# Hybrid Hyena, mLSTM and S5 block on one core: S5 tables at two places, modulation on ScalarE, and the output order

## The chip, the cores and the metric

The kernel runs on one core of one Trainium2 chip, as one launch. The core has TensorE (matmuls and transposes), VectorE, ScalarE, GpSimd and SyncE, each with its own instruction queue that is worked off in order, and DMA queues that SyncE, ScalarE and GpSimd issue transfers on. The metric is the device time of one launch in microseconds (us); smaller is better. In the rows of the profile PE is TensorE's matmuls, PEld its weight loads, DVE VectorE, ACT ScalarE, POOL GpSimd and SP SyncE.

## The reference

One layer of a hybrid backbone, for 256 latent tokens `x` and 256 context tokens `ctx`, width D = 2048, all in fp32. Cut to what the change touches:

```
mod_l = split(silu(c) @ w_mod + b_mod, 6);  mod_c = split(silu(c_ctx) @ w_mod + b_mod, 6)
h_ctx = ctx * (1 + mod_c[1]) + mod_c[0];    h_lat = x * (1 + mod_l[1]) + mod_l[0]
hy, qk, v, o, gates, u, mg = split(h @ w_in)          # widths 2304, 1536, 768, 768, 16, 768, 6144
y_hy = hyena(hy)          # short convolution, then two long convolutions
y_ml = mlstm(qk, v, gates, o)
# S5: 48 groups of 16 channels, 64 complex states each, both directions, context first, then latents
s[t] = A_bar * s[t-1] + B_bar @ u[t];   y[t] = Re(C @ s[t])
y_s5 = z * sigmoid(z @ glu_w + glu_b),  z = gelu(y + d * u)
merged = sigmoid(mg[0]) * (y_hy @ w_hy_out) + sigmoid(mg[1]) * (y_ml @ w_ml_out) + sigmoid(mg[2]) * (y_s5 @ w_s5_out)
x = layer_norm(alpha * x + mod_l[2] * (merged @ w_out))
out = layer_norm(alpha * x + mod_l[5] * mlp(x * (1 + mod_l[4]) + mod_l[3]))
```

S5 is computed by chunks of 8 tokens, 64 chunks in all. `WA` holds the powers of A_bar times B_bar, which take the inputs of a chunk to its end state (the inject); the scan runs over the 64 chunks; `QD` holds the powers times C, which take a chunk's start state to its outputs; `KD` holds the lag kernels (C, powers, B), which take the inputs of a chunk to its own outputs.

## The kernel before

Each large matmul is fp32 made of three products of a rounded format: the weight chunk `wr` (128 x 1024, loaded on SyncE's queue, four buffers) is split by ScalarE into `wh` (a copy, L190) and by VectorE into `wl` (a subtraction, L194), three buffers each; `mm` (L211) then issues 24 matmuls of 256 columns for a chunk, 48 where it serves latents and context. A tile scheduler, which has a cost model of its own, sets the order in which each engine's instructions stand; the code gives it priorities by its own order. Side work is written as generators: `with_side` starts one, `chunk_done` advances each by its rate at every chunk, `drain` runs one out.

The stages, by the times of the profiled execution:

- First stage (`phase0`, scope `p0a`, to about 235 us): eight `mod_block`s multiply `w_mod` by `silu(c)` (matmuls `px`, L406) into `modc`. `h_group` (L435) modulates x and ctx in place, 32 pieces of 128 x 256 on VectorE, and splits them into the operands `t`. K steps of `w_in` run between. On the side: `s5_params` (L443) computes A_bar's powers `s5pq` and B_bar, and `s5_tables` the tables. `powers` makes them with broadcast products (L536, L537) and one sum (L538), direction 0 on VectorE and direction 1 on GpSimd; `s5Q` is C's table, `s5w` B's. L564 multiplies `s5Q` by B (`s5bb`) for the lag kernels. QD, KK and WA go to memory.
- pA, to about 582 us: at its start a copy `gate` on GpSimd and `s5_spread`, which writes KK into the 8 block-diagonal places of KD; then V, Q, mLSTM, U, O columns, with the Hyena filters and the later modulation (`mod_late`: `mac`, L1181) beside them. `u_consume` puts U into UD (memory) and `uT`.
- pB, to about 980 us: 6 steps of the Hyena columns `hy`, `s5_inject` (WA and UD loaded on ScalarE's queue, L634 matmuls, results to `S`), then `s5_scan` as a side: 63 steps of four GpSimd operations (L652 to L655) on 128 x 96, each needing the one before. Beside it stand 36 `hy` steps with their short convolutions (L741, L743) and 32 steps of the gate columns `mg`. `s5_output` (L687 on) needs the scan's end; 48 gate-column steps, and the gated unit `s5_glu`.
- pC: `hyena` with the last 16 gate-column steps, and the merges; then `w_out`, norms, and the MLP to 2044 us.

## Time and profile before

| | |
|---|---|
| median of 3 runs | 2034.3 us (2031.83 to 2036.18) |
| the profiled execution | 2046.25 us, its span 2044.3 us |
| granted TensorE clock, mean over the span | 0.964 |
| busy in the span: TensorE, VectorE, ScalarE, GpSimd | 1885.0, 1342.6, 797.7, 473.4 us |
| DMA | 455.92 MB, 223 GB/s |

TensorE is busy 92% of the span, so most stages are bound by its matmuls. A stage with another limit shows where TensorE's share falls; so the profile is read by stretches below. A wait is put down to the engine and line that released it last. Where transfers are the subject, the DMA share and GB/s of a stretch count, and what SyncE's queue waited for.

### The profile page before, as it was taken

What the parts mean: (1) busy time and instruction counts of PE and PEld (TensorE: products, weight loads), DVE (VectorE), ACT (ScalarE), POOL (GpSimd) and SP (SyncE); (2) the same over time, 40 slices, a digit from 0 to 9 for tenths busy, and PEclk for the clock granted to TensorE, in tenths of its full rate; (3) what the DMA queues carried; (4) which work ended last, traced back from release to release, by engine and by line L of the source; (5) the groups of instructions that cost most, each with busy time, mean ns of one, the idle gap of its engine ahead of it and who ended that gap; (6) DMA issues with size and microseconds to landing.
All of it is one profiled execution on the core that took longest, in us unless ns stands there. A gap on an engine that the chain in (4) does not pass through costs nothing.

```text
span 2044.3 us, 34693 instructions
## 1 busy us (share of the span) xinstructions
PE 1885.0 (92%) x13945; PEld 1716.5 (84%) x13945; DVE 1342.6 (66%) x1842; ACT 797.7 (39%) x1079; POOL 473.4 (23%) x654
## 2 busy tenths in 40 slices
PE   4787899999999896999889998899999999999996
PEld 1555888898998896999769977899989899998986
DVE  8789876655876564455777767866655555555556
ACT  1233333324544332534333443544343334444332
POOL 4777311000015997000343400500000000000001
PEclk8898899999999898999999999999999999999998
DMA  8798667766698675777756876577765566666653
GB/s 311 262 299 285 195 203 221 228 199 184 206 318 272 211 242 172 262 251 243 270 183 217 278 249 218 174 248 229 244 208 190 189 185 181 184 185 230 190 187 115
DMA packets 255200, 455.92 MB, mean 223 GB/s; under 512 B 28789, under 2 KB 75541, under 8 KB 253504
## 3 DMA queue, kind: packets, MB, share of 16 engines
q1 hardware_dynamic: 221824, 382.43, 59.0%
q0 software_dynamic: 12384, 44.54, 6.2%
q10 hardware_dynamic: 20832, 26.75, 3.9%
q8 instruction: 109, 1.79, 0.4%
q14 instruction: 51, 0.42, 0.1%
HBM read 424.75 MB, written 32.05 MB: 223 GB/s over the span
## 4 chain that ended last, share of the span: by engine, by line
PE 64%; DVE 14%; DMA 8%; POOL 8%; issue 4%; ACT 1%; ACTq 0%; POOLq 0%; DVEq 0%; SPq 0%
PE mm L211 57%; DMA wr<-in_w_mod_dram 4%; PE aux L211 4%; DVE wl L194 4%; POOL sc L654 2%; POOL sc L653 2%; POOL t L655 2%; POOL sc L652 2%; DVE t L194 1%; DMA wr<-in_w_in_dram 1%; DVE ty L435 1%; ACT wh L190 1%; DVE mac L1181 1%; DVE s5t L537 1%; DMA s5wq<-WA 1%
## 5 line engine op out<-in xcount | busy, mean ns | idle before, releaser
L211 PE MATMUL mm<-t,wh 128*128 128x256 f32 x5888 | 1102.7, 288 | 24.8 <-ACT wh L190 12.6
L211 PEld LDWEIGHTS mm<-t,wh 128*128 128x128 f32 x5888 | 933.7, 194 | 46.6 <-ACT wh L190 13.9
L194 DVE TENSOR_TENSOR wl<-wr,wh 128x1024 fp32r<-128x1024 f32 (+1 forms) x517 | 657.0, 1277 | 381.6 <-ACT wh L190 380.7
L211 PE MATMUL mm<-t,wl 128*128 128x256 f32 x2944 | 850.1, 289 | 23.3 <-DVE wl L194 23.0
L190 ACT ACTIVATE wh<-wr 128x1024 fp32r<-128x1024 f32 (+1 forms) x517 | 546.4, 1058 | 807.9 <-PE mm L211 577.6
L211 PEld LDWEIGHTS mm<-t,wl 128*128 128x128 f32 x2944 | 571.4, 194 | 37.4 <-DVE wl L194 29.4
L1181 DVE SCALAR_TENSOR_TENSOR mac<-wr,vecs,mac 128x512 f32<-128x512 f32 x240 | 186.8, 778 | 152.7 <-DMA wr<-in_w_mod_dram 150.0
L211 PE MATMUL mm<-wh,t 128*128 128x512 f32 (+1 forms) x960 | 249.3, 349 | 1.7 <-ACT wh L190 1.7
L211 PEld LDWEIGHTS mm<-wh,t 128*128 128x128 f32 x960 | 169.7, 191 | 25.6 <-ACT wh L190 2.7
L211 PE MATMUL mm<-wl,t 128*128 128x512 f32 (+1 forms) x480 | 169.2, 352 | 5.2 <-DVE wl L194 5.2
L211 PE MATMUL mm<-wh,ff 128*128 128x512 f32 (+1 forms) x576 | 155.3, 358 | 0.0
L211 PEld LDWEIGHTS mm<-wh,ff 128*128 128x128 f32 x576 | 101.8, 188 | 17.6
L211 PEld LDWEIGHTS mm<-wl,t 128*128 128x128 f32 x480 | 91.6, 191 | 21.7 <-DVE wl L194 10.5
L211 PE MATMUL mm<-wl,ff 128*128 128x512 f32 (+1 forms) x288 | 103.0, 357 | 0.0
L1403 POOL DMA_DIRECT2D t<-in_ln_g_dram x1 | 0.5, 535 | 358.8 <-PE mm L211 358.8
L211 PE MATMUL mm<-ty,wh 128*128 128x256 f32 x384 | 74.1, 291 | 0.0
L211 PE MATMUL mm<-ty,wl 128*128 128x256 f32 x192 | 57.0, 297 | 6.7 <-DVE wl L194 6.7
L211 PEld LDWEIGHTS mm<-ty,wh 128*128 128x128 f32 x384 | 61.6, 195 | 0.9
L211 PEld LDWEIGHTS mm<-wl,ff 128*128 128x128 f32 x288 | 54.2, 188 | 8.8
L1192 POOL DMA_DIRECT2D mrow<-b x8 | 4.0, 502 | 227.8 <-DVE b L1190 227.8
L211 PE MATMUL aux<-t,t 128*128 128x384 f32 (+3 forms) x160 | 48.8, 422 | 8.0 <-DVE t L1147 3.5
L406 PE MATMUL px<-wr,b 128*32 128x512 f32 x128 | 40.3, 714 | 12.9 <-DVE s5t L335 10.7
(389 smaller groups left out, 1813.6 us busy)
## 6 DMA issues: line engine op xcount, KB each, us to landing
wr<-in_w_ff_dram SPq DMA_DIRECT2D x256, 512.0 KB, 3.9
wr<-in_w_in_dram SPq DMA_DIRECT2D x192, 512.0 KB, 4.7
wr<-in_w_mod_dram SPq DMA_DIRECT2D x160, 512.0 KB, 4.8
wr<-in_w_out_dram SPq DMA_DIRECT2D x32, 512.0 KB, 4.9
wh<-in_w_mod_dram SPq DMA_DIRECT2D x16, 512.0 KB, 6.2
wl<-in_w_mod_dram SPq DMA_DIRECT2D x16, 512.0 KB, 7.8
QD<-s5Q POOLq DMA_DIRECT2D x24, 256.0 KB, 4.9
WA<-s5wa ACTq DMA_DIRECT2D x24, 256.0 KB, 5.2
```

The lines of the kernel that those rows point to most:

```text
L190: return self.nc.scalar.activation(out, in_, f, bias=bias, scale=scale)
L194: self.nc.vector.tensor_sub(lo, x, hi.bitcast(F32))
L211: self.nc.tensor.matmul(out, lhsT, rhs, start=start, stop=stop, skip_group_check=True)
L406: nc.tensor.matmul(ps[o:o + 32], self.st[:, k, :], raw[:, kk, :], start=k < 4, stop=k >= KT - 4, skip_group_check=True, tile_position=(0, o))
L435: self.nc.vector.tensor_scalar(h[:, j], h[:, j], self.modc[:, 16 + k, m:m + 1], self.modc[:, k, m:m + 1], op0=ALU.mult, op1=ALU.add)
L537: e.tensor_mul(t[:, :, s], bcp(s), bcm(1))
L652: v.tensor_mul(t1, self.a8[:, 0], S[:, :, :, :, n - 1])
L653: v.tensor_mul(t2, self.a8[:, 1], S[:, :, ::-1, :, n - 1])
L654: v.tensor_add(t1, t1, S[:, :, :, :, n])
L655: v.tensor_add(S[:, :, :, :, n], t1, t2)
L1181: v.scalar_tensor_tensor(acc, x, c, acc, op0=ALU.mult, op1=ALU.add)
L1192: nc.gpsimd.dma_start(self.mrow[which // 3:which // 3 + 1, o:o + 512], brow)
```

## The change

`h_group` modulates on ScalarE (an Identity activation with a per-partition scale and bias). `s5_tables` is split in two. `s5_into` stays in the first stage: the powers of B, their transposes and WA. The new `s5_tables` makes Q, the lag kernels and KK in a new scope `pT`, beside the Hyena and gate columns, at the rate 0.6, and at its end calls `s5_spread`, which no longer stands in pA. All powers are on VectorE, four state pairs at a time: products of 512 (B) or 576 (C), and one sum of twice that. B and the powers `s5pq` are written to memory (SB, PQ) and loaded again. QD and KK are written on ScalarE's queue.

`s5_inject` takes one pair at a time: 24 loads of WA of 256 KB on GpSimd's queue, four buffers. UD, KD, QD and the new UL, which keeps U in memory in place of `uT`, are loaded on GpSimd's queue too. mLSTM's `st_all` becomes four smaller tiles, so that it no longer waits for the tile that the modulated inputs hold.

The order changes too: 4 `hy` steps before the inject rather than 6; then the scan and the tables beside 36 `hy` and 24 gate-column steps, the tables run out, 8 more gate-column steps, `s5_output` at the rate 0.4 with 24 steps beside it, and 40 steps left for the Hyena stage.

```diff
@@ h_group
-                    self.nc.vector.tensor_scalar(h[:, j], h[:, j], self.modc[:, 16 + k, m:m + 1],
-                                                 self.modc[:, k, m:m + 1], op0=ALU.mult, op1=ALU.add)
+                    self.act(h[:, j], h[:, j], AF.Identity, bias=self.modc[:, k, m:m + 1],
+                             scale=self.modc[:, 16 + k, m:m + 1])
@@ s5_params, its end
+        nc.gpsimd.dma_start(self.SB, B.rearrange("p a b c -> p (a b c)"))
+        nc.gpsimd.dma_start(self.PQ, pq.rearrange("p a b c -> p (a b c)"))
@@ powers
-        e = self.nc.vector if d == 0 else self.nc.gpsimd
...
+        v = self.nc.vector
+        q = slice(24 * d + 4 * ct, 24 * d + 4 * ct + 4)
...
         for s in range(2):
-            e.tensor_mul(out[:, :, s], bcp(1 + s), bcm(0))
-            e.tensor_mul(t[:, :, s], bcp(s), bcm(1))
-        e.tensor_add(out, out, t)
+            v.tensor_mul(out[:, s], bcp(1 + s), bcm(0))
+            v.tensor_mul(t[:, s], bcp(s), bcm(1))
+        v.tensor_add(out, out, t)
+    def s5_into(self):
+        for ct in range(CT):
+            wt = []
+            for d in range(2):
+                w = self.t(self.br, [P, 2, 4, P], "s5w", 4)
+                self.powers(w.rearrange("p s q (l c) -> p s q l c", c=16), self.s5B, d, ct, d, LC)
+                wt.append(w)
+            yield
+            for i in range(4):
+                wa = self.t(self.br, [P, 4, P], "s5wa", 2)
+                pt = self.aux([P, 4, P])
+                for d in range(2):
+                    for s in range(2):
+                        self.tr(pt[:, 2 * d + s, :], wt[d][:, s, i])
+                self.act(wa, pt)
+                nc.scalar.dma_start(self.WA[ct, :, i], wa)
+                if i % 2:
+                    yield
     def s5_tables(self):
+        nc.gpsimd.dma_start(B.rearrange("p a b c -> p (a b c)"), self.SB)
+        nc.gpsimd.dma_start(self.pq.rearrange("p a b c -> p (a b c)"), self.PQ)
+        nc.gpsimd.dma_start(C, self.I["s5c"])
         for ct in range(CT):
...
+            for d in range(2):
+                Q = self.t(self.br, [P, 2, 4, 144], "s5Q", 2)
+                self.powers(Q.rearrange("p s q (l c) -> p s q l c", c=16), C, d, ct, 0, 9)
+                bb = self.t(self.br, [P, 2, 4, 32], "s5bb", 2)
+                nc.gpsimd.memset(bb, 0.0)
...
-                    nc.gpsimd.dma_start(self.QD[ct, d, :, 2 * half:2 * half + 2], Q[:, :, :, o:o + P])
+                nc.scalar.dma_start(self.QD[ct, d], Q[:, :, :, o:o + P])
...
-            nc.gpsimd.dma_start(self.KK[ct], kk.rearrange("p l c -> p (l c)"))
+            nc.scalar.dma_start(self.KK[ct], kk.rearrange("p l c -> p (l c)"))
+        self.s5_spread()
@@ s5_inject
-            wa = self.t(self.br, [P, 4, 4, P], "s5wq", 2)
-            nc.scalar.dma_start(wa, self.WA[ct])
...
+            for i in range(4):
+                wa = self.t(self.br, [P, 4, P], "s5wa", 4)
+                nc.gpsimd.dma_start(wa, self.WA[ct, :, i])
@@ mlstm
-        st_all = self.t32(F32, (P, 4, HEADS, T))
-            s_sb = st_all[:, sb]
+            s_sb = self.ty()[:, :HEADS, :]
@@ run
-                    yield from self.s5_tables()
+                    yield from self.s5_into()
...
-                gate = self.t(self.sm, [P, LC], "gate", 1)
-                nc.gpsimd.tensor_copy(gate[:LC], self.kT[:LC, 2, :LC])
-                nc.gpsimd.dma_start(self.KD[:, 0, 0, 0, 0].unsqueeze(1), gate[:LC, 0:1])
-                self.s5_spread()
...
-                self.run_steps(hy, 6)
-                self.s5_inject()
+                self.run_steps(hy, 4)
+                for _ in self.s5_inject():
+                    pass
                 self.sides[1][1] = 0.3
                 self.with_side(self.s5_scan(), 2)
+                self.with_side(self.s5_tables(), 0.6, 2)
                 self.run_steps(hy, 36)
-                self.run_steps(steps, 32)
-                self.with_side(self.s5_output(), 0.6)
-                self.run_steps(steps, 48)
+                self.run_steps(steps, 24)
+                self.drain(2)
+            with self.scope("pB") as self.br:
+                self.run_steps(steps, 8)
+                self.with_side(self.s5_output(), 0.4)
+                self.run_steps(steps, 24)
```

On VectorE in the first stage, around a modulated group, the order before is this (`s5Q`, `s5w` and `s5t` are the tables and their products, `ty` the inputs, `t_19` and `t_20` the split operands):

```order
L537 TENSOR_TENSOR s5t_31_129<-s5pq_189,s5B_121 128x2x128 x2
L415 TENSOR_TENSOR modc_101<-px_457,vecs_93 128x8
L538 TENSOR_TENSOR s5w_418<-s5w_418,s5t_31_129 128x512
L435 TENSOR_SCALAR ty_107<-ty_107,modc_101 128x256 x2
L435 TENSOR_SCALAR ty_109<-ty_109,modc_101 128x256 x2
L435 TENSOR_SCALAR ty_108<-ty_108,modc_101 128x256 x2
L435 TENSOR_SCALAR ty_110<-ty_110,modc_101 128x256 x2
L537 TENSOR_TENSOR s5t_31_129<-s5pq_189,s5C_122 128x2x144 x2
L194 TENSOR_TENSOR t_19_102<-ty_107,t_19_102 128x512
L194 TENSOR_TENSOR wl_559<-wr_556,wh_558 128x1024
```

And after it:

```order
L539 TENSOR_TENSOR s5w_360<-s5w_360,s5t_130 128x1024
L538 TENSOR_TENSOR s5t_130<-s5pq_190,s5B_124 128x512 x2
L539 TENSOR_TENSOR s5w_366<-s5w_366,s5t_130 128x1024
L194 TENSOR_TENSOR t_22_105<-ty_110,t_22_105 128x512
L194 TENSOR_TENSOR t_23_106<-ty_112,t_23_106 128x512
L538 TENSOR_TENSOR s5t_130<-s5pq_190,s5B_124 128x512 x2
L194 TENSOR_TENSOR wl_513<-wr_510,wh_512 128x1024
L194 TENSOR_TENSOR t_22_105<-ty_111,t_22_105 128x512
L194 TENSOR_TENSOR t_23_106<-ty_113,t_23_106 128x512
L537 TENSOR_TENSOR s5w_416<-s5pq_190,s5B_124 128x512 x2
L537 TENSOR_TENSOR s5w_422<-s5pq_190,s5B_124 128x512 x2
```

The modulations and `s5Q` are gone from there, and a `powers` operation is now of 512 or 1024 elements.

On GpSimd the scan before stands nearly alone; HX is a write of the Hyena columns:

```order
L652 TENSOR_TENSOR sc_748_5894<-t_713_5520 128x96
L653 TENSOR_TENSOR sc_749_5895<-t_713_5520 128x96
L654 TENSOR_TENSOR sc_748_5894<-sc_748_5894,t_713_5520 128x96
L655 TENSOR_TENSOR t_713_5520<-sc_748_5894,sc_749_5895 128x96
L1094 DMA HX_90<-b_911_6730 256x1x128
L652 TENSOR_TENSOR sc_750_5900<-t_713_5520 128x96
```

After it, at its step 38, the lag kernels are written (KD) and the tables of the output loaded:

```order
L666 TENSOR_TENSOR sc_879_6299<-t_643_4946 128x96
L667 TENSOR_TENSOR sc_880_6300<-t_643_4946 128x96
L611 DMA KD_73<-KK_92 48x16x128 x5
L668 TENSOR_TENSOR sc_879_6299<-sc_879_6299,t_643_4946 128x96
L611 DMA KD_73<-KK_92 48x16x128 x3
L686 DMA s5wq_8283<-QD_77 128x2x1024
L686 DMA s5wq_8408<-QD_77 128x2x1024
L1226 DMA MG_74<-mg_7321 128x512
L1226 DMA MG_74<-mg_7324 128x512
L669 TENSOR_TENSOR t_643_4946<-sc_879_6299,sc_880_6300 128x96
L666 TENSOR_TENSOR sc_885_6340<-t_643_4946 128x96
```

The KD writes and the loads now stand between two operations of one step, with all later steps behind them.

On VectorE beside the scan, before:

```order
L194 TENSOR_TENSOR wl_6564<-wr_6561,wh_6563 128x1024
L194 TENSOR_TENSOR wl_6610<-wr_6607,wh_6609 128x1024
L741 SCALAR_TENSOR_TENSOR b_836_6335<-b_826_6303,vecs_93,b_836_6335 128x4x63
L743 SCALAR_TENSOR_TENSOR b_836_6335<-b_826_6303,vecs_93,b_836_6335 128x4x63
L194 TENSOR_TENSOR wl_6652<-wr_6649,wh_6651 128x1024
L642 TENSOR_TENSOR t_713_5520<-aux_5626,one_10_81 128x2x32 x4
L642 TENSOR_TENSOR t_713_5520<-aux_5649,one_10_81 128x2x32 x4
L194 TENSOR_TENSOR wl_6737<-wr_6734,wh_6736 128x1024
L1181 SCALAR_TENSOR_TENSOR mac_6472<-wr_6776,vecs_93,mac_6472 128x512
```

After, with the tables of C (`s5Q`) in that stretch:

```order
L539 TENSOR_TENSOR s5Q_5911<-s5Q_5911,s5t_5383 128x1152
L757 SCALAR_TENSOR_TENSOR b_819_5945<-b_812_5923,vecs_96,b_819_5945 128x4x63
L194 TENSOR_TENSOR wl_6508<-wr_6505,wh_6507 128x1024
L538 TENSOR_TENSOR s5t_5383<-s5pq_5382,s5C_5381 128x576 x2
L759 SCALAR_TENSOR_TENSOR b_819_5945<-b_812_5923,vecs_96,b_819_5945 128x4x63
L537 TENSOR_TENSOR s5Q_6442<-s5pq_5382,s5C_5381 128x576 x2
L539 TENSOR_TENSOR s5Q_6153<-s5Q_6153,s5t_5383 128x1152
L194 TENSOR_TENSOR wl_6554<-wr_6551,wh_6553 128x1024
```

Products and sums of `powers` now stand among the weight splits and the convolutions.

## Rows read from the trace of the kernel before

**Rows 1.** Stretches: PE, PEld, DVE, ACT, POOL busy (count), PEclk, DMA share, GB/s.

```profile
0.00:200.00 200.00, 143.54 (x1000) 93.76 (x1002) 168.40 (x294) 56.38 (x158) 133.97 (x184) 0.87 0.86 289
20.00:40.00 20.00, 13.09 (x66) 3.69 (x66) 19.45 (x59) 3.32 (x14) 8.49 (x15) 0.74 0.98 360
660.00:808.00 148.00, 120.35 (x963) 118.26 (x963) 77.13 (x72) 47.16 (x55) 139.90 (x232) 0.93 0.65 209
980.00:1142.00 162.00, 141.01 (x1011) 130.24 (x1010) 124.94 (x146) 57.30 (x73) 65.26 (x67) 0.95 0.68 227
```

**Rows 2.** What SyncE's DMA queue waits for, 0 to 300 us: total, times, longest.

```profile
SPq L200 <- PE px L406: 59.6, 22, 13.6
SPq L200 <- DVE wl L194: 50.5, 16, 8.9
```

**Rows 3.** Lines L536, L537, L538 (`powers`), 0 to 245 us: DVE, then POOL busy.

```profile
0.00:245.00 245.00, 36.04 (x48) 40.49 (x48) 0.87 0.82 275
...
0.00:245.00 245.00, 35.10 (x48) 38.16 (x48) 0.87 0.82 275
...
0.00:245.00 245.00, 28.82 (x24) 34.44 (x24) 0.87 0.82 275
```

**Rows 4.** VectorE's groups by form, 0 to 245 us: count, busy, mean ns.

```profile
L194 DVE TENSOR_TENSOR wl<-wr,wh 128x1024 fp32r<-128x1024 f32 x15 | 22.9, 1525 | 0.0
L435 DVE TENSOR_SCALAR ty<-ty,modc 128x256 f32<-128x256 f32 x32 | 21.6, 741 | 0.1
```

**Rows 5.** Timeline of VectorE, first stage, no GpSimd operation beside: start, duration.

```profile
35.70 0.69 DVE L538 TENSOR_TENSOR s5w<-s5w,s5t 128x512 f32<-128x512 f32 x1
...
203.86 1.22 DVE L194 TENSOR_TENSOR wl<-wr,wh 128x1024 fp32r<-128x1024 f32 x1
```

**Rows 6.** ScalarE's groups by form, 0 to 245 us: count, busy, mean ns.

```profile
L190 ACT ACTIVATE t<-ty 128x512 fp32r<-128x512 f32 x16 | 10.1, 630 | 15.8 <-DVE ty L435 13.7 <-DMA wr<-in_w_mod_dram 2.1
...
L190 ACT ACTIVATE t<-ty,vecs 128x512 f32<-128x512 f32 x6 | 4.6, 808 | 6.2 <-DVE ty L1460 3.1 <-DMA WA<-s5wa 3.1
```

**Rows 7.** Timeline of TensorE: last modulation matmul, first K step, first gate matmul.

```profile
200.04 0.60 PE L406 MATMUL px<-wl,b 128*32 128x512 f32 x2
...
209.86 0.79 PE L211 MATMUL mm<-t,wh 128*128 128x256 f32 x2 [4.64 <-ACT t L190]
...
234.81 0.63 PE L211 MATMUL px<-t,b 128*32 128x256 f32 x4
```

**Rows 8.** Page, part 6: DMA issues, count, size, median us to landing.

```profile
QD<-s5Q POOLq DMA_DIRECT2D x24, 256.0 KB, 4.9
WA<-s5wa ACTq DMA_DIRECT2D x24, 256.0 KB, 5.2
```

**Rows 9.** Timeline of GpSimd: first and last scan operation, and an undisturbed step.

```profile
634.38 0.44 POOL L652 TENSOR_TENSOR sc<-t 128x96 f32<-128x96 f32 x1 [3.18 <-DVE t L642]
...
660.14 0.44 POOL L652 TENSOR_TENSOR sc<-t 128x96 f32<-128x96 f32 x1
...
661.95 0.44 POOL L652 TENSOR_TENSOR sc<-t 128x96 f32<-128x96 f32 x1
...
808.30 0.40 POOL L655 TENSOR_TENSOR t<-sc,sc 128x96 f32<-128x96 f32 x1
```

**Rows 10.** Waits of all engines, 634 to 860 us: total, times, longest.

```profile
PE aux L687 <- POOL sc L652: 15.8, 1, 15.8
```

**Rows 11.** GpSimd's groups by form, 634 to 809 us.

```profile
L1211 POOL DMA_DIRECT2D MG<-mg x8 | 4.6, 573 | 0.1
```

**Rows 12.** Timeline during the scan: GpSimd beside `mac`, beside `wl`; those `wl`.

```profile
714.97 0.89 POOL L653 TENSOR_TENSOR sc<-t 128x96 f32<-128x96 f32 x1
715.82 1.42 POOL L654 TENSOR_TENSOR sc<-sc,t 128x96 f32<-128x96 f32 x1
...
715.48 2.85 DVE L194 TENSOR_TENSOR wl<-wr,wh 128x1024 fp32r<-128x1024 f32 x2
```

**Rows 13.** Timeline of GpSimd: a product of `powers`, no VectorE operation beside.

```profile
72.18 0.68 POOL L536 TENSOR_TENSOR s5Q<-s5pq,s5C 128x288 f32<-128x288 f32 x1
```

More of the change, by code (lines that the diff above doesn't have):

```diff
@@ L445, in s5_params @@
         nc.gpsimd.dma_start(par, I["s5a"])
-        B, C = (self.t(self.br, [P, 2, 48, 16], tag, 1) for tag in ("s5B", "s5C"))
+        B = self.t(self.br, [P, 2, 48, 16], "s5B", 1)
         nc.gpsimd.dma_start(B, I["s5b"])
-        nc.gpsimd.dma_start(C, I["s5c"])
         yield
         are, aim, lg = par[:, 0, :], par[:, 1, :], par[:, 2, :]
-        self.work = [self.t(self.br, [P, 1152], f"s5t{d}", 1) for d in range(2)]
-        tmp = self.slices(self.work[0][:, :1104].rearrange("p (a n) -> p a n", n=48))
+        self.work = self.t(self.br, [P, 1152], "s5t", 1)
+        tmp = self.slices(self.t(self.br, [P, 23, 48], "s5tmp", 1))
         dt_, mag, ph, cs, sn = (tmp(x) for x in ("dt", "mag", "ph", "cs", "sn"))
@@ L503, in s5_params @@
         br, bi = B[:, 0], B[:, 1]
-        w1, w2 = (self.work[1][:, 384 * i:384 * i + 384].rearrange("p (q c) -> p q c", c=16) for i in range(2))
+        w1, w2 = (self.work[:, 384 * i:384 * i + 384].rearrange("p (q c) -> p q c", c=16) for i in range(2))
         for d in range(2):
@@ L544, in s5_tables @@
         v = nc.vector
+        B, C = (self.t(self.br, [P, 2, 48, 16], tag, 1) for tag in ("s5B", "s5C"))
+        self.pq = self.t(self.br, [P, 3, 48, 9], "s5pq", 1)
+        self.work = self.t(self.br, [P, 1152], "s5t", 1)
+        nc.gpsimd.dma_start(B.rearrange("p a b c -> p (a b c)"), self.SB)
+        nc.gpsimd.dma_start(self.pq.rearrange("p a b c -> p (a b c)"), self.PQ)
+        nc.gpsimd.dma_start(C, self.I["s5c"])
+        yield
         for ct in range(CT):
             pk = self.aux([P, 2, P])
[L547 to L583 removed]
@@ new lines, in s5_tables @@
+            for d in range(2):
+                q = slice(24 * d + 4 * ct, 24 * d + 4 * ct + 4)
+                Q = self.t(self.br, [P, 2, 4, 144], "s5Q", 2)
+                self.powers(Q.rearrange("p s q (l c) -> p s q l c", c=16), C, d, ct, 0, 9)
+                bb = self.t(self.br, [P, 2, 4, 32], "s5bb", 2)
+                nc.gpsimd.memset(bb, 0.0)
+                for h in range(2):
+                    for s in range(2):
+                        self.act(bb[64 * h:64 * h + 64, s, :, 16 * h:16 * h + 16],
+                                 B[64 * h:64 * h + 64, s, q, :], scale=1.0 - 2.0 * s)
+                yield
+                l0 = 0 if d == 0 else 16
+                for s in range(2):
+                    for p in range(4):
+                        nc.tensor.matmul(pk[32 * p:32 * p + 32, d, :], bb[:, s, p, :], Q[:, s, p, l0:l0 + P],
+                                         start=d == 0 and s == 0, stop=s == 1, skip_group_check=True,
+                                         tile_position=(0, 32 * p))
+                o = 16 - l0
+                nc.scalar.dma_start(self.QD[ct, d], Q[:, :, :, o:o + P])
@@ L624, in s5_inject @@
         for ct in range(CT):
[L625 to L643 removed]
+            u = self.s5_u(ct, self.b2([P, 8, NCH]))
+            for i in range(4):
+                wa = self.t(self.br, [P, 4, P], "s5wa", 4)
+                nc.gpsimd.dma_start(wa, self.WA[ct, :, i])
+                pi = self.aux([P, 4, NCH])
+                for x in range(4):
+                    for h in range(2):
+                        r = slice(64 * h, 64 * h + 64)
+                        nc.tensor.matmul(pi[r, x, :], wa[:, x, r], u[:, 2 * i + h, :], start=x == 0, stop=True,
+                                         skip_group_check=True, tile_position=(0, 64 * h))
+                g = 4 * ct + i
+                self.act(self.S[:, 0, :, g, :], pi[:, 0:2, :])
+                for half in range(2):
+                    o = 32 * half
+                    nc.vector.tensor_mul(self.S[:, 1, :, g, o:o + 32], pi[:, 2:4, o:o + 32][:, :, ::-1],
+                                         self.one1.unsqueeze(2).to_broadcast([P, 2, 32]))
+                yield
     def s5_scan(self):
@@ L687, in s5_output @@
                         self.nc.tensor.matmul(py[o:o + 64, p // 2, :], xb[:, p, d, s].rearrange("p g j -> p (g j)"),
-                                              Q[:, d, p, s, :], start=p < 2 and d == 0 and s == 0, stop=False,
+                                              Q[:, d, s, p, :], start=p < 2 and d == 0 and s == 0, stop=False,
                                               skip_group_check=True, tile_position=(0, o))
```

92 lines of the change are left out of this document (23 added, 69 removed).

## The prediction

> **What bounds the kernel now.** The first view is the busy time by stretch [rows 1]. In the first stage, to 200 us, TensorE is busy 143.5 of 200 us, VectorE 168.4, and DMA has 0.86 of its share: it leans on VectorE and on the transfers. The second view is what SyncE's weight loads wait for [rows 2]: 59.6 us for a `px` matmul on TensorE and 50.5 us for `wl` on VectorE, which release their buffers. So a stall of VectorE is a stall of the transfers too. Later TensorE is nearly always busy, but for one place: from 660 to 808 it has 120.35 of 148 us, while GpSimd has 139.9 [rows 1]. That is the S5 scan, 63 dependent steps of four GpSimd operations; the first matmul of `s5_output` waits 15.8 us for it [rows 10]. Two stretches decide here: the first stage, and the scan. The rest is a row of matmuls that the change only shifts.
>
> **First stage: VectorE.** The power operations cost VectorE 36.0 + 35.1 + 28.8 = 100 us and the modulation 21.6 us [rows 3, 4]; GpSimd has as much again. Only the powers of B stay, all on VectorE: 12 tables, each of four products of 512 and one sum of 1024. With GpSimd idle beside it, a 512 sum took 0.69 us and a 1024 split 1.22 us [rows 5]; 48 x 0.69 + 12 x 1.22 = 48 us. Gone are 52 + 22 = 74 us, and the rest gets cheaper without GpSimd's products: `wl` averages 1.525 us here [rows 4] against 1.22 alone, 15 x 0.3 = 4.6 us. VectorE falls from 168 us of 200 to about 90 and no longer bounds.
>
> ScalarE takes 32 modulations of 256 elements. The form isn't in the trace: `t<-ty` of 512 costs 0.630 us and 0.808 with a per-partition operand [rows 6]. It is at most that 0.81 and hardly under half of 0.63; I take 0.60, so 19 us, on an engine that has 56 us in 200 [rows 1] and hands 96 small `s5bb` copies on to a later stage. It is hidden, except for the last eight, which stand before the last K steps: 8 x 0.60 = 4.8 us, where VectorE needed 8 x 0.67 or more. Nothing gained or lost.
>
> The Trainium skill, "ScalarE: Activation LUTs", Rules for kernel authors, speaks against this part: it sends a multiply or an add to VectorE. By that page's timing (186 ns + 0.833 ns an element + about 93 ns for each pointer) one modulation would be an estimated 0.59 us on ScalarE; the crowded VectorE of this stage needed 0.674 us (21.6 / 32). The rule holds for a VectorE that has time; here the sum stays the same by either.
>
> **First stage: what is late next.** The transfers. To 200.04 us, the last modulation matmul [rows 7], 289 GB/s x 200 us = 57.8 MB moved [rows 1]. About 23 of 24 QD writes of 256 KB (6.0 MB) and the load of C (0.8 MB) go; two small writes (0.79 + 0.66 MB) come: 52.4 MB. At which rate? The mean is 289; the stretch from 20 to 40 us had 360 [rows 1]. At 300 the last matmul comes at 175 us, at 360 at 146; I take 330, 159 us, nearer to the top because VectorE's share of the waits goes and TensorE's stays [rows 2]. From there to the gates it is now 234.81 - 200.04 = 34.8 us [rows 7], of it a wait of 4.64 us for the modulated tile, which stands behind power products on VectorE; I take 4 off. **Gain 45 us**, bounds 25 (300 GB/s, nothing off behind) and 58 (360, all off).
>
> **The way to the scan.** From the gates on the order is the same until U. Ahead of the last inject matmul stand 113 fewer `mm` matmuls (two `hy` steps and some `mod` work): at 120.35 / 963 = 0.125 us each [rows 1], 14 us. The inject now loads 24 pieces of 256 KB on GpSimd's queue into four buffers, instead of six of 1 MB on ScalarE's. Pieces of this size land in 4.9 us from GpSimd's queue and 5.2 from ScalarE's [rows 8]. Six rounds of four with no overlap would be 6 x 5 = 30 us, but `hy` steps stand between the matmuls and a load follows each release; I take 5, bounds 0 and 15. Behind these loads on GpSimd's queue wait the HX writes of `hy`, wanted only in the hyena stage. mLSTM runs during U instead of O, both full of matmuls: nothing. So the scan starts 45 + 14 - 5 = 54 us earlier, at 580 instead of 634.4 us [rows 9].
>
> The Trainium skill, "SBUF — State Buffer", SBUF: two separate sides, has a rule against moving loads to GpSimd's queue: their descriptors can't be written while certain VectorE operations hold a port that both share. By it six rounds would each wait for at most one `wl`, an estimated 6 x 1.4 = 8 us in all; the first stage's pieces show no such lateness with VectorE as busy (4.9 against 5.2 us).
>
> **The scan, which now has the tables beside it.** It ran from 634.4 to 808.7 us, 174.3 us. An undisturbed step is 1.81 us (660.14 to 661.95) [rows 9], and 63 of them 114 us. Other work on GpSimd was 11.4 us, eight MG writes 4.6 of it [rows 11]. The other 49 us are lost to VectorE: a scan operation takes 1.42 us with `wl` beside it and 0.89 with `mac` [rows 12], against 0.44 alone [rows 9]. Each `wl` thus blocks for up to 0.97, I take 0.90; a `mac` for 0.37; a short convolution, which is half a `mac`, for 0.2. Between the last inject and the first output operation stand 44 `wl`, 28 `mac` and 14 convolutions: 39.6 + 10.4 + 2.8 = 52.8, against the 49 seen: a factor of 0.93.
>
> After the change the order has 41 `wl`, 29 `mac` and 26 convolutions there: 36.9 + 10.7 + 5.2 = 52.8 again. New are 38 products of 576 and 10 sums of 1152. By `wl`'s ratio (0.90 of 1.22 us), a product of some 0.76 us (0.69 by size) blocks 0.55 and a sum 1.0. The first stage hints at less: GpSimd's 288 product took 0.68 us alone and 40.5 / 48 = 0.84 on average beside VectorE's [rows 3, 13], so 0.16 more. Between 0.16 and 0.55 I take 0.42, nearer to `wl`, because the scan's operations are as short as the ones it slows; 16 us for the products, 10 for the sums: (52.8 + 26) x 0.93 = 73 us. GpSimd's own extras grow from 11.4 to about 28 us: 14 HX and 6 MG writes, 12 memsets, 8 KD writes, 8 loads, at the 0.573 of MG and more. One memset in step 1 waits for a table matmul, about 4. **The scan: 114 + 28 + 73 + 4 = 219, say 220 us, 46 longer.** Bounds: 197 (products at 0.1, extras at half) and 241 (products and sums strictly one after the other with the scan, and the memset at 8).
>
> TensorE has 1163 `mm` and 96 table matmuls in that stretch, 145 + 9 us, instead of 1133 `mm`: of 220 us it waits some 50, in stalls on the tables or at the first output matmul, instead of 15.8 there. VectorE's work there is about 155 of 220 us, so it isn't the bound. One new wait stands inside the scan: the KD writes, which need the last table, stand on GpSimd's queue behind step 37, and all later steps behind them. VectorE's work up to the last table sum is 79 us by the single durations (29 + 14 for the tables, 16 `wl`, 13 `mac`, 23 convolutions), some 110 with GpSimd beside it, and the table's way to memory some 8; the scan is at step 37 after 67 + 16 + 46 = 129 us. I take no wait.
>
> **Behind it.** By the output's start 1133 + 113 - 1163 = 83 fewer `mm` are done: 83 x 0.125 = 10 us more to do. 40 gate-column steps instead of 16 are left for the hyena stage, where TensorE now idles 162 - 141 = 21 us [rows 1]; they fill a part, 5 us.
>
> **Sum:** -45 - 14 + 5 + 46 + 10 - 5 = -3 us. The profiled execution took 2046.25 us, so 2043; it lies 12 us above the median of the runs, 2034.3, on which I put the same difference: **2031 us**. What the first stage gives, the scan takes.
>
> **Rivals.**
> *The scan takes more (slower).* While VectorE has a table operation, GpSimd stands still for its whole length: 38 x 0.76 + 10 x 1.37 (1.22 by size) = 42 us instead of 24, so 237 us of scan and 2048 us. It turns the sign once the scan exceeds some 223 us. For it: `wl` costs 0.90 of 1.22; against: the first stage's products. Chance 0.14. The Trainium skill, "SBUF — State Buffer", SBUF: two separate sides, states such an exclusive lock for the whole instruction; the rows agree for `wl` beside a scan operation (1.42 us, two `wl` in 2.85) [rows 12].
> *The first stage stays slow (slower).* Transfers go on at 300 GB/s, since TensorE releases the buffers: gain 27, 2049 us. For it: the 59.6 us [rows 2]; against: VectorE delays that TensorE work too. Chance 0.11.
> *Cheap tables, quick loads (faster).* Products cost the scan 0.16, so 210 us; transfers run at 350: gain 53; 2013 us. For it: [rows 13] and the 360 of [rows 1]. Chance 0.25.
> *GpSimd waits inside the scan (slower).* The tables come later than step 37, since TensorE, ScalarE and VectorE wait in turn for a table's two buffers; 129 us against 118 leaves little. At 15 us of waiting, part of the scan's lost time, it is 2046 us. Chance 0.10.
>
> **How the numbers follow.** My own case has 0.40 and runs from 2018 to 2044. Within 0.2% (4 us, about what a measurement can tell from no change) is 0.13 of it, faster 0.18, slower 0.09. With the rivals: faster 0.18 + 0.25 = 0.43; same 0.13 and 0.05 of the edges of the three rivals above the forecast, 0.18; slower 0.39. The range, 2006 to 2054, takes in the centres of all cases and leaves out their outer parts on both sides, together 0.2.
>
> **What would show it.** Right: the last modulation matmul at 155 to 165 us with VectorE at half load before it; the scan's start near 580 us; a scan near 220 us, with operations of 0.9 us and more beside table operations; some 50 us of idle TensorE between inject and output. Wrong: DMA still at 290 GB/s in the first stage; a scan under 200 or over 240 us; a first output matmul that waits for a load and not for the scan.

## The result and the profile after

The changed kernel takes 2064.0 us (median of four, 2054.5 to 2066.7) against 2033.2 for the kernel before on the same chip (median of four, one execution more than in the table before): 1.0141 of it, 95% interval 1.0106 to 1.0176. It is slower, by some 30 us, and outside the range that was given. The profiled execution took 2066.65 us, its span is 2064.9.

The stretches of the changed kernel (engines in the order PE, PEld, DVE, ACT, POOL; then granted clock, DMA share, GB/s), to be read against [rows 1]:

```profile
0.00:170.00 170.00, 129.75 (x840) 85.64 (x840) 95.94 (x211) 51.23 (x85) 6.48 (x28) 0.89 0.91 313
...
587.00:640.00 53.00, 39.42 (x325) 35.55 (x324) 45.87 (x53) 18.44 (x52) 50.49 (x74) 0.79 0.54 158
640.00:720.00 80.00, 59.19 (x442) 54.97 (x442) 61.48 (x69) 27.38 (x50) 73.11 (x105) 0.80 0.61 195
720.00:800.00 80.00, 63.19 (x501) 62.28 (x499) 34.43 (x32) 21.92 (x23) 72.94 (x119) 0.91 0.81 276
```

The first stage did what it should: VectorE is at 96 of 170 us and the transfers run at 313 GB/s. The trouble stands beside the scan. There TensorE is busy only 74 to 79% of the time, and its granted clock is 0.79 to 0.80, a mixture of the two levels (2.4 and 1.2 GHz), while the tables last. In [rows 1] it had 0.93.

The timeline of the changed kernel, against [rows 7, 9]: the last modulation matmul, the first and last scan operation, the first matmul of the output:

```profile
169.38 1.03 PE L406 MATMUL px<-wl,b 128*32 128x512 f32 x4
...
586.93 0.44 POOL L666 TENSOR_TENSOR sc<-t 128x96 f32<-128x96 f32 x1 [2.73 <-DVE t L655]
...
801.90 0.39 POOL L669 TENSOR_TENSOR t<-sc,sc 128x96 f32<-128x96 f32 x1
...
820.43 0.55 PE L703 MATMUL aux<-s5wq,b 128*64 128x128 f32 x6
```

The scan starts 47.5 us earlier than before and ends 6.4 us earlier; it now takes 215.4 us. But the output's first matmul, which came together with the scan's end before, comes 18 us after it, and waits for nothing then: it is simply TensorE's turn so late. What TensorE waited for between 587 and 821 us (in answer to [rows 10]; total, times, longest):

```profile
PE mm L211 <- ACT wh L190: 42.7, 10, 10.2
PE mm L211 <- DVE wl L194: 8.2, 8, 1.8
PE px L214 <- DVE b L759: 3.5, 2, 2.3
```

No wait of a TensorE instruction for the scan itself is left in the list. Of the 54 us, 51 are waits for the two halves of the weight split. But two of the ten waits for `wh`, 7.6 and 10.2 us, come after 720 us; the last table operation ends at 702. In both a copy on ScalarE stands ahead of `wh` in the queue and waits, first for a write of MG to land, then for the scan's last operation (ScalarE's timeline):

```profile
749.65 0.60 ACT L190 ACTIVATE mg<-mm 128x512 f32<-128x512 f32 x1 [9.31 <-DMA MG<-mg]
...
800.36 1.03 ACT L190 ACTIVATE b<-t 64x128 f32<-64x128 f32 x4 [15.73 <-POOL t L669]
```

So the longest of the waits, 10.2 us, is a wait for the scan after all, one step removed.

For the experiments I sum this up in two numbers. I take the starts of TensorE's matmuls in a row and subtract from each distance what the columns take at the higher clock (0.12 us for 256 columns). A rest of more than 0.35 us is *idle* time; a smaller one is *stretched* time, most of it matmuls at the lower clock (0.21 us apart in place of 0.12). The first pair of numbers runs from the last modulation matmul to the first inject matmul, the second from the last inject matmul to the first output matmul; the inject itself is in neither. Idle and stretched time together are what TensorE loses. The wait of that output matmul for the scan is left out: it is 12 to 22 us in the kernels with -1 in the column before.

| kernel | last modulation matmul | scan start | scan, us | first output matmul after the scan's end | idle, stretched: first stage to inject | idle, stretched: inject to output | time / before |
|---|---|---|---|---|---|---|---|
| before | 200.1 | 634.4 | 174.3 | -1 | 14, 49 | 18, 8 | 1 |
| after | 169.8 | 586.9 | 215.4 | 18 | 10, 48 | 59, 31 | 1.0141 |
| e1_zero_once | 174.3 | 594.6 | 206.5 | 20 | 11, 48 | 56, 27 | 1.0116 |
| e2_mod_vector | 158.5 | 578.3 | 215.7 | 18 | 11, 48 | 62, 27 | 1.0065 |
| e4_zero_once_late_out | 170.6 | 589.9 | 206.6 | 53 | 10, 48 | 54, 29 | 1.0138 |
| e5_no_products | 165.6 | 604.2 | 201.2 | -1 | 10, 48 | 22, 14 | 1.0046 |
| e7_tables_first | 162.7 | 698.8 | 185.1 | 7 | 29, 61 | 32, 10 | 1.0051 |
| e8_wa_buffers | 162.4 | 578.9 | 215.8 | 18 | 11, 47 | 60, 29 | 1.0082 |
| e9_before_mod_scalar | 192.8 | 615.8 | 175.5 | -1 | 7, 49 | 15, 7 | 0.9926 |
| e10_output_earlier | 170.0 | 585.3 | 213.9 | -1 | 11, 46 | 44, 28 | 1.0174 |
| e11_products_twice | 170.2 | 588.4 | 214.8 | 63 | 10, 46 | 78, 30 | 1.0249 |
| e12_before_mod_zero | 188.9 | 623.8 | 175.6 | -1 | 14, 52 | 14, 9 | 0.9967 |
| e13_tables_gpsimd | 161.1 | 740.9 | 186.3 | -1 | 49, 64 | 10, 7 | 1.0133 |
| e14_filled_not_made | 169.5 | 579.1 | 199.4 | -1 | 11, 46 | 16, 16 | 0.9928 |
| e16_before_all_vector | 182.8 | 608.1 | 174.2 | -1 | 9, 49 | 16, 7 | 0.9864 |

All times in it are of the profiled executions; the ratios are of the runs, each against runs of the kernel before on the same chip. (In the kernels that make the tables before the inject, e7 and e13, the column "first stage to inject" holds them.)

### The profile page after: what moved, and what is told of

Same layout as the page of the kernel before. It is cut to its first block, busy times and chain, and to the rows that moved or that the text cites. A ratio compares the mean times of both kernels' runs of the same rounds, so it can differ in the third digit from the quotient of the medians.

```text
span 2064.9 us, 34589 instructions
## 1 busy us (share of the span) xinstructions
PE 1896.5 (92%) x13945; PEld 1726.2 (84%) x13945; DVE 1315.0 (64%) x1810; ACT 802.3 (39%) x1062; POOL 382.8 (19%) x548
## 5 line engine op out<-in xcount | busy, mean ns | idle before, releaser
L211 PE MATMUL mm<-t,wh 128*128 128x256 f32 x5888 | 1125.3, 292 | 64.2 <-ACT wh L190 52.7
L211 PEld LDWEIGHTS mm<-t,wh 128*128 128x128 f32 x5888 | 948.2, 197 | 93.1 <-ACT wh L190 58.0
L194 DVE TENSOR_TENSOR wl<-wr,wh 128x1024 fp32r<-128x1024 f32 x517 | 648.0, 1257 | 467.2 <-ACT wh L190 465.9
L190 ACT ACTIVATE wh<-wr 128x1024 fp32r<-128x1024 f32 x517 | 545.4, 1057 | 830.7 <-PE mm L211 580.2
L211 PEld LDWEIGHTS mm<-t,wl 128*128 128x128 f32 x2944 | 578.9, 197 | 39.3 <-DVE wl L194 31.4
L1196 DVE SCALAR_TENSOR_TENSOR mac<-wr,vecs,mac 128x512 f32<-128x512 f32 x240 | 188.9, 787 | 105.2 <-DMA wr<-in_w_mod_dram 102.3
L211 PE MATMUL mm<-wh,ff 128*128 128x512 f32 (+1 forms) x576 | 153.9, 356 | 0.0
L668 POOL TENSOR_TENSOR sc<-sc,t 128x96 f32<-128x96 f32 x63 | 48.5, 769 | 0.0
```

Source lines behind the costliest of these rows:

```text
L190: return self.nc.scalar.activation(out, in_, f, bias=bias, scale=scale)
L194: self.nc.vector.tensor_sub(lo, x, hi.bitcast(F32))
L211: self.nc.tensor.matmul(out, lhsT, rhs, start=start, stop=stop, skip_group_check=True)
L668: v.tensor_add(t1, t1, S[:, :, :, :, n])
L1196: v.scalar_tensor_tensor(acc, x, c, acc, op0=ALU.mult, op1=ALU.add)
```

## The experiments

**Which wait makes TensorE late.** In the changed kernel ScalarE waits long for two things on GpSimd (its waits from 587 to 821 us, and VectorE's for it):

```profile
ACT s5bb L190 <- POOL s5bb L581: 55.3, 9, 11.0
DVE wl L194 <- ACT wh L190: 51.2, 23, 10.6
...
ACT b L190 <- POOL t L669: 15.7, 1, 15.7
```

Each `s5bb` copy needs a memset that stands between two scan steps on GpSimd, and `wh` copies stand behind it on ScalarE. So the first theory was ScalarE's queue, against VectorE's time as a rival.

```diff
+        bbs = [self.t(self.br, [P, 2, 4, 32], f"s5bb{d}", 1) for d in range(2)]
+        for bb in bbs:
+            v.memset(bb, 0.0)
...
-                bb = self.t(self.br, [P, 2, 4, 32], "s5bb", 2)
-                nc.gpsimd.memset(bb, 0.0)
+                bb = bbs[d]
```

> The changed kernel with one edit: the two s5bb tiles are zeroed once on VectorE ahead of the scan, so that no memset of them stands between the scan's operations on GpSimd. Theory 1 (ScalarE's queue): the 55.3 us in which ScalarE waits for these memsets, with the weight copies wh queued behind, are what made TensorE late; TensorE's 42.7 us of waiting for wh between 587 and 821 us fall under 20, the first output matmul comes within 5 us of the scan's end, and the time is 2036 to 2048 us against some 2064. Rival 2 (VectorE's table operations make wl late, and the scan long): TensorE waits for wl instead, and the time stays at 2058 to 2068.

Measured: 1.0116 [1.0089, 1.0142]. The theory fell. The waits for memsets are gone, the scan is 9 us shorter, and TensorE loses almost as much (56 and 27 us):

```profile
PE mm L211 <- ACT wh L190: 23.6, 9, 7.9
PE mm L211 <- DVE wl L194: 22.6, 13, 11.4
...
ACT wh L190 <- DMA wr<-in_w_in_dram: 59.2, 23, 6.1
```

Its waiting is now half for `wl`, and `wh` waits for weights, whose buffers VectorE frees. The memset was the last wait of a chain, not its cause.

In e4 the output stands 12 steps later on top of that:

```diff
-                self.run_steps(steps, 8)
-                self.with_side(self.s5_output(), 0.4)
-                self.run_steps(steps, 24)
+                self.run_steps(steps, 20)
+                self.with_side(self.s5_output(), 0.6)
+                self.run_steps(steps, 12)
```

> e1_zero_once, and s5_output 12 gate-column steps later (20 of them before it instead of 8, 12 beside it instead of 24): 1435 mm matmuls stand between the last inject and the first output matmul instead of 1163, about 34 us more. Theory 1: with the stalls gone TensorE would wait for the scan, and the later output fills that wait: 2012 to 2030 us. Rival 2: TensorE is late anyway, nothing is to be filled, and the time is that of e1_zero_once within 6 us.

Measured: 1.0138 [1.0113, 1.0163]; nothing was to be filled, and the output comes 53 us after the scan. Moved the other way, the output starts with the scan's end again:

```diff
-                self.run_steps(steps, 8)
                 self.with_side(self.s5_output(), 0.4)
-                self.run_steps(steps, 24)
+                self.run_steps(steps, 32)
```

> The changed kernel with s5_output 8 gate-column steps earlier (none before it, 32 beside it). Theory 2: the first output matmul then waits for the scan and starts with it near 802 us instead of 820, but TensorE's idle time up to there stays 55 to 75 us, and the time within 0.4% of the changed kernel. Rival 5 (the place of the output makes the loss): 0.7% or more faster.

Measured: 1.0174 [1.014, 1.0209], within 0.4% of the changed kernel. On the shorter way to the output 44 and 28 us are lost; with the 15 us in which the output's own matmul waits for the scan the idle time is 59 us, as in the changed kernel. The place of the output is not the cause.

**The products.** e5 takes the products and sums away; Q is two tiles zeroed once.

```diff
+        Qs = [self.t(self.br, [P, 2, 4, 144], f"s5Q{d}", 1) for d in range(2)]
...
-                Q = self.t(self.br, [P, 2, 4, 144], "s5Q", 2)
-                self.powers(Q.rearrange("p s q (l c) -> p s q l c", c=16), C, d, ct, 0, 9)
+                Q = Qs[d]
```

> The changed kernel without the products and sums of the tables beside the scan (Q is zeros, which leaves the lag kernels and the readout of S5 wrong); the memsets on GpSimd stay in the scan. Theory 1: the scan is 24 us shorter (190 us), but ScalarE still waits 35 us or more for the memsets, TensorE 30 or more for wh, and the time falls by 10 to 20 us. Rival 2: the stalls go with the products: TensorE's waits for wh and wl fall under 20, and the time falls by 25 us or more.

Measured: 1.0046 [1.0024, 1.0068]; TensorE's loss falls from 59 and 31 to 22 and 14 us, as the rival said, but the time falls only by 19 us, where the rival had 25 or more and theory 1 had 10 to 20. With free tiles the QD writes came early, ScalarE waited for two of them during the inject (11.8 and 11.2 us), and TensorE was idle for 27 us there, so the size was open. e14 keeps the tiles' turn and makes each by one fill in place of five operations:

```diff
-                self.powers(Q.rearrange("p s q (l c) -> p s q l c", c=16), C, d, ct, 0, 9)
+                v.memset(Q, 0.0)
```

> The changed kernel with each table beside the scan filled with zeros by one VectorE instruction instead of four products and a sum (lag kernels and readout of S5 are then wrong): some 40 us of VectorE less, and the tables' tiles, matmuls, copies and writes keep their places, which e5_no_products did not. Theory 2: TensorE's idle and slow time between the last inject and the first output matmul falls from 89 to 35 to 55 us, its time in the inject stays, and the time falls by 25 to 45 us, to 0.992 to 1.002 of the kernel before. Rival 1 (ScalarE's waits for the memsets on GpSimd, which stay): 70 us or more stay, the time falls by less than 15 us.

Measured: 0.9928 [0.9902, 0.9953]. Memsets, copies, table matmuls and writes are all still beside the scan, and of the loss 16 and 16 us are left, besides the output's wait for the scan. The granted clock is higher as well; the same time window of the changed kernel and of e14:

```profile
587.00:821.00 234.00, 179.56 (x1393) 170.15 (x1393) 153.93 (x166) 77.50 (x137) 199.79 (x302) 0.83 0.67 216
```

```profile
587.00:821.00 234.00, 203.65 (x1780) 196.14 (x1779) 131.80 (x158) 93.16 (x159) 186.29 (x302) 0.92 0.81 273
```

Its timeline is the one that the prediction had drawn for the changed kernel, an output that waits for the scan's last step:

```profile
778.11 0.39 POOL L669 TENSOR_TENSOR t<-sc,sc 128x96 f32<-128x96 f32 x1
...
777.50 2.40 PE L703 MATMUL aux<-s5wq,b 128*64 128x128 f32 x20 [16.46 <-POOL sc L666]
```

So making the tables beside the scan costs 1.0141 - 0.9928 = 2.1%, some 43 us. On the profiles 34 of them lie between the last inject and the first output matmul (234 and 200 us); another 9 lie ahead of that, where e14's order also has 32 `mm` matmuls fewer before the last inject matmul. The opposite, every product made twice:

```diff
-                self.powers(Q.rearrange("p s q (l c) -> p s q l c", c=16), C, d, ct, 0, 9)
+                for _ in range(2):
+                    self.powers(Q.rearrange("p s q (l c) -> p s q l c", c=16), C, d, ct, 0, 9)
```

> The changed kernel with the products and sums of the tables beside the scan made twice, some 52 us more of VectorE (48 x 0.75 and 12 x 1.35, the durations of e7_tables_first). Theory 2, as it stands after e7_tables_first (VectorE's time is what is short, wherever the tables stand): TensorE's idle and slow time between the last inject and the first output matmul grows by 35 to 60 us over the 89 us of the changed kernel, the time by 30 to 60 us. Rival 1 (ScalarE's waits for GpSimd and for buffers make the stalls): under 15 us more.

Measured, on two executions: 1.0249 [1.0223, 1.0275], 22 us more than the changed kernel; 78 and 30 us are lost instead of 59 and 31, 18 more where theory 2 had 35 to 60. That lies between the theories: the second set costs half as much as the first. The table operations, which end at 702 us in the changed kernel, run on to 825 there, spread thinner and partly behind the scan's end; that this is the reason is argued, not shown.

**Is it the scan, or VectorE's time?** e7 makes the tables ahead of the inject, beside gate columns, with no scan on GpSimd (and the modulation on VectorE, from e2 below):

```diff
+                self.with_side(self.s5_tables(), 0.9, 2)
+                self.run_steps(steps, 36)
+                self.drain(2)
                 self.run_steps(hy, 4)
...
-                self.with_side(self.s5_tables(), 0.6, 2)
                 self.run_steps(hy, 36)
-                self.run_steps(steps, 24)
-                self.drain(2)
...
+                self.run_steps(steps, 26)
+                self.with_side(self.s5_output(), 0.5)
+                self.run_steps(steps, 14)
```

> e2_mod_vector with the tables moved out of the scan: they are made beside 36 gate-column steps, before the inject, while GpSimd has no scan; the scan then stands beside 36 Hyena and 26 gate-column steps, the output beside 14 more, 20 steps are left. Theory 2 (products and sums on VectorE beside the scan make wl late, TensorE stalls and its clock falls): TensorE's idle time between the last inject and the first output matmul falls from 59 to some 20 us and the slow part from 30 to 10, with at most 20 us of new stalls beside the tables; the scan is back at 175 to 185 us, and the time is 2.0 to 3.5% under e2_mod_vector, 1 to 3% faster than the kernel before. Rival 4 (the tables cost TensorE the same wherever they stand, since VectorE is short of time beside any columns): within 1% of e2_mod_vector.

Measured: 1.0051 [1.0035, 1.0066] against e2's 1.0065: rival 4. The scan is back at 185 us, and the way to the output loses 32 and 10 us, 47 less than in e2. But ahead of the inject, where the tables stand now, 31 us are lost anew (29 and 61 us for e2's 11 and 48). Where the rest went, with the order changed as well, is not settled. The tables' stretch and VectorE's groups there:

```profile
520.00:600.00 80.00, 68.01 (x620) 62.24 (x621) 76.99 (x98) 31.98 (x74) 6.09 (x16) 0.96 0.89 277
```

```profile
L194 DVE TENSOR_TENSOR wl<-wr,wh 128x1024 fp32r<-128x1024 f32 x30 | 36.7, 1222 | 12.8 <-ACT wh L190 12.8
L1196 DVE SCALAR_TENSOR_TENSOR mac<-wr,vecs,mac 128x512 f32<-128x512 f32 x32 | 23.9, 747 | 2.1 <-DMA wr<-in_w_mod_dram 2.0
L537 DVE TENSOR_TENSOR s5Q<-s5pq,s5C 128x576 f32<-128x576 f32 x24 | 17.1, 753 | 1.0 <-DMA QD<-s5Q 1.0
L538 DVE TENSOR_TENSOR s5t<-s5pq,s5C 128x576 f32<-128x576 f32 x24 | 17.1, 752 | 0.0
L539 DVE TENSOR_TENSOR s5Q<-s5Q,s5t 128x1152 f32<-128x1152 f32 x12 | 16.2, 1351 | 0.0
```

VectorE is busy 77.0 of 80 us: the splits, `mac` and 50 us of tables fill it. e13 gives the tables to GpSimd, which is idle there (`powers` takes the engine; 40 gate-column steps beside them):

```diff
-                self.powers(Q.rearrange("p s q (l c) -> p s q l c", c=16), C, d, ct, 0, 9)
+                self.powers(Q.rearrange("p s q (l c) -> p s q l c", c=16), C, d, ct, 0, 9, nc.gpsimd)
```

> e7_tables_first with the tables' products and sums on GpSimd, which is idle before the scan (some 97 us of it), beside 40 gate-column steps. Theory 2 (VectorE's time): VectorE falls from 95 to 100% busy beside the tables to under 85%, TensorE's idle and slow time before the inject falls by 20 us or more, and the time by 0.8 to 1.6% under e7_tables_first, to 0.99 of the kernel before. Rival 6 (the tables' matmuls, copies and writes themselves disturb TensorE): within 0.4% of e7_tables_first.

Measured: 1.0133 [1.0105, 1.0161], 0.8% worse than e7, which neither theory had. Its stretch beside the tables, and the groups of both engines there:

```profile
520.00:640.00 120.00, 90.84 (x776) 85.59 (x774) 116.42 (x63) 38.70 (x81) 116.14 (x74) 0.91 0.79 241
```

```profile
L194 DVE TENSOR_TENSOR wl<-wr,wh 128x1024 fp32r<-128x1024 f32 x25 | 61.7, 2492 | 3.1 <-ACT wh L190 3.1
L1196 DVE SCALAR_TENSOR_TENSOR mac<-wr,vecs,mac 128x512 f32<-128x512 f32 x29 | 52.9, 1822 | 0.5
```

```profile
L538 POOL TENSOR_TENSOR s5t<-s5pq,s5C 128x576 f32<-128x576 f32 x22 | 42.3, 1941 | 0.1
L537 POOL TENSOR_TENSOR s5Q<-s5pq,s5C 128x576 f32<-128x576 f32 x22 | 36.4, 1674 | 0.0
L539 POOL TENSOR_TENSOR s5Q<-s5Q,s5t 128x1152 f32<-128x1152 f32 x12 | 35.7, 2976 | 0.2
```

VectorE has no table operation and is as full as before: a `wl` takes 2.49 us in place of 1.22, a `mac` 1.82 in place of 0.75. Both engines are busy 116 of 120 us. At e7's durations VectorE's 25 `wl` and 29 `mac` would take 52 us, so more than half of its busy time is put on by GpSimd's operations; for products of 576 on GpSimd no run here has a price without VectorE beside it. So it seems to be the time of this pair that is short, not that of VectorE alone, a reading made after the result; e16 below tests it.

**The modulation.** Back on VectorE in the changed kernel:

```diff
-                    self.act(h[:, j], h[:, j], AF.Identity, bias=self.modc[:, k, m:m + 1],
-                             scale=self.modc[:, 16 + k, m:m + 1])
+                    self.nc.vector.tensor_scalar(h[:, j], h[:, j], self.modc[:, 16 + k, m:m + 1],
+                                                 self.modc[:, k, m:m + 1], op0=ALU.mult, op1=ALU.add)
```

> The changed kernel with the modulation back on VectorE. Theory 1: VectorE has room in the first stage now, so the last modulation matmul stays at 169 +- 4 us and the time within 5 us of 2064. Rival 3 (ScalarE's modulation took back part of the first stage's gain): the gates come 5 us earlier or more and the time falls by as much.

Measured: 1.0065 [1.0039, 1.009], 15 us less; the last modulation matmul comes at 158.5, 11 us earlier. ScalarE's longest waiting in the first stage of the changed kernel was for writes of WA, with only two `s5wa` tiles; e8 has four, in `s5_into`:

```diff
-                wa = self.t(self.br, [P, 4, P], "s5wa", 2)
+                wa = self.t(self.br, [P, 4, P], "s5wa", 4)
```

> The changed kernel with four s5wa tiles in the first stage instead of two. Theory 3a (ScalarE's queue in the first stage: copies s5wa that wait for WA writes, 37.6 us, hold up the modulation and wh behind them, which VectorE's modulation does not suffer): the last modulation matmul comes 6 us or more earlier than 169.8, the time falls by 0.3 to 0.7%. Rival 3b (the modulations' own length on ScalarE, 16 us, and their order): no change beyond 0.2%.

Measured: 1.0082 [1.0054, 1.0109], 12 us less. The wait, in the changed kernel and then with four tiles:

```profile
ACT s5wa L190 <- DMA WA<-s5wa: 37.6, 11, 5.9
```

```profile
ACT s5wa L190 <- DMA WA<-s5wa: 3.0, 3, 1.6
```

So the modulations and the `t` copies behind them stood in ScalarE's queue behind copies that waited for a write. In the kernel before, the modulation on ScalarE alone (e2's diff the other way round):

> The kernel before with the modulation on ScalarE, the one part alone. If VectorE bounds the first stage as the prediction said, it gains: 21.6 us of VectorE go, and the last modulation matmul comes 8 us or more before 200; the time falls by 0.3 to 0.8%. If ScalarE's order is what matters (theory 3a), modulations wait there behind s5bb and s5wa copies, the stage gains nothing or loses up to 10 us.

Measured: 0.9926 [0.9901, 0.995]. There it helps by 15 us, the last modulation matmul coming 7 us earlier, where 8 or more were expected. In e12, the two `s5bb` tiles of the old `s5_tables` are also zeroed once, ahead of its loop:

> The kernel before with the modulation on ScalarE (e9_before_mod_scalar) and with its two s5bb tiles zeroed once instead of 24 memsets on GpSimd, which ScalarE waited 18.6 us for: 0.0 to 0.3% under e9_before_mod_scalar's 0.9926 of the kernel before, if that wait delays the modulations behind it on ScalarE; no change if the transfers bound the stage.

Measured: 0.9967 [0.9953, 0.9981]. That is a miss: 0.4% slower than e9. The stage ends 4 us earlier, the scan starts 8 us later than in e9; why the K steps and gates then took longer I did not settle.

**The tables where they were, on one engine.** e16 is e9 with all powers on VectorE.

```diff
-        e = self.nc.vector if d == 0 else self.nc.gpsimd
+        e = self.nc.vector
```

> The kernel before with the modulation on ScalarE and with all powers on VectorE, none on GpSimd, all tables staying in the first stage: VectorE gets 48 products of 288 and 48 of 256 and 24 sums more, some 58 us at durations without GpSimd beside, and loses what GpSimd's operations held it up. If the two engines take turns on the same operands' memory (as wl at 2.49 us beside GpSimd's products in e13_tables_gpsimd says), the first stage is not longer than in e9_before_mod_scalar: the last modulation matmul at 180 to 195 us, the time within 0.5% of e9_before_mod_scalar, or below it. If GpSimd's half was real help, VectorE's 164 us of 200 grow past the stage: last modulation matmul after 200 us, the time 0.5% or more above e9_before_mod_scalar.

Measured: 0.9864 [0.9834, 0.9893], 28 us faster than the kernel before, the best of all. VectorE's six groups of powers in its first stage:

```profile
L536 DVE TENSOR_TENSOR s5Q<-s5pq,s5C 128x288 f32<-128x288 f32 x48 | 19.8, 452 | 3.5 <-DMA QD<-s5Q 3.2 <-PE aux L564 0.3
L537 DVE TENSOR_TENSOR s5t<-s5pq,s5C 128x288 f32<-128x288 f32 x48 | 19.5, 450 | 0.1
...
L537 DVE TENSOR_TENSOR s5t<-s5pq,s5B 128x256 f32<-128x256 f32 x48 | 18.0, 417 | 0.1
L538 DVE TENSOR_TENSOR s5Q<-s5Q,s5t 128x576 f32<-128x576 f32 x24 | 17.7, 751 | 0.1
L536 DVE TENSOR_TENSOR s5w<-s5pq,s5B 128x256 f32<-128x256 f32 x48 | 17.4, 417 | 3.1 <-PE aux L214 3.1
L538 DVE TENSOR_TENSOR s5w<-s5w,s5t 128x512 f32<-128x512 f32 x24 | 16.2, 684 | 0.2
```

Together 108.6 us for all of them; half of them had cost VectorE 100 us beside GpSimd's other half [rows 3].

## Why the prediction was wrong, point by point

- *First stage, VectorE.* Right. The powers of B took 45 us (in e2: 0.685, 0.687 and 1.222 us each) for the 48 worked out, `wl` 1.22 us, and VectorE's load fell to 96 of 170 us.
- *Modulation on ScalarE, hidden.* Wrong. Its length was right (0.586 us for 0.60), its place was not: it stood behind `s5wa` copies waiting 37.6 us for their writes. The step that named the cover looked at how busy ScalarE is and not at what waits in its queue. The cost is 12 to 15 us (e8, e2); with either edit the last modulation matmul comes at 162.4 or 158.5, where the prediction had 159. The rule of the Trainium skill, "ScalarE: Activation LUTs", Rules for kernel authors, which favours VectorE here, turned out right for the changed kernel and wrong for the kernel before (e9); what decided, as far as e8 and its waits show, was what stood in each engine's queue.
- *Transfers.* 313 GB/s to 170 us, not 330, and 53.2 MB, not 52.4: 170 us. A gain of 36.5 us up to the gates instead of 45.
- *The way to the scan.* Start at 586.9 for 580.4: the stage gave 8.5 us less, the way behind it 2 us more (11 for 9). Loads of WA on GpSimd's queue landed in 4.8 us (median of 24, page of the changed kernel), so the rule of the Trainium skill, "SBUF — State Buffer", SBUF: two separate sides, about descriptors held up by VectorE, which the page states for VectorE's 2-port modes and the prediction applied to `wl`, cost nothing that the runs show.
- *The scan.* 215.4 us for 220, about right in the sum. Against e14's fills (199.4 us) the products and sums cost it 16 us, where the prediction had 24. The rival of a wait at KD didn't come: 2.4 us for the MG writes that follow the KD writes, nothing at KD itself.
- *TensorE beside the scan: this is the step that failed.* The prediction gave it 145 + 9 us of work, found VectorE at 155 of 220 us, "so it isn't the bound", and let TensorE wait "some 50" us in the slack (its own figures, 220 - 154, leave 66). VectorE's amount of work was right, 153.9 us, and so were the waits: 54 us. But TensorE's own work took 180 us, since the granted clock was 0.79 to 0.91 and not 0.93, and 180 + 54 = 234 us is more than the scan's 215. So the term that the prediction put at nothing, TensorE late for the output, measured 18 us behind the scan's end; e14, without the products, has it at -1 us. The average over 220 us hid how the work lies: in the 115 us up to 702, where the tables end, VectorE is busy for 94 us and GpSimd for 110, with 51 us of table operations, 16 splits, `mac` and 23 convolutions on VectorE. (The prediction itself had "some 110 with GpSimd beside it" for this and used it only for the KD wait.) That this crowding makes the splits late is argued from e1, e5 and e14; 18 of the 54 us are the two late waits behind copies on ScalarE shown above.
- *Behind it.* 10.9 us, for 5: the 83 matmuls cost their 10 us and the later gate columns filled nothing.
- *The sum*, on the profiles: -47.5 (start) + 41.1 (scan) + 19.1 (output behind the scan's end, from -1.0 to 18.1) + 10.9 - 3.1 (behind `w_out`, not part of the change) = 20.5 us, for the 20.6 seen. The forecast was -3: of the 23.5 us between them 19.1 are the output, 6.5 the start and 5.9 the work behind, with 4.9 off for the scan and 3.1 for what lies behind `w_out`. The medians lie 31 us apart, as the profiled execution of the kernel before was 13 us above its median and that of the changed kernel 3; this part of the miss is in no term of the sum.
- *The rivals.* "The scan takes more" had the right side and named the right pair of engines, but on the wrong victim: not GpSimd's scan but VectorE's splits, and through them TensorE.

Behind all that stands one thing that the prediction did not ask: what the moved work costs where it goes. In the first stage TensorE had 56 us of 200 to spare, and the tables of C there cost some 13 to 20 us (e16's last modulation matmul at 182.8, against 169.8 in the changed kernel and 162.4 in e8, which have them elsewhere; the three differ in smaller things too); beside column work, where TensorE is the bound, they cost some 43 us (e14).
